# A hybrid decoder block on one core: the query and key products in plain form, and four smaller moves in the order of the work

## The chip, the core and the metric

One core of a Trainium2 chip. The metric is the device time of one launch in microseconds (us); lower is better. Several runs are made of a kernel, and their median is its time. The profiled execution is one more run, taken by the hardware profiler. TensorE is written PE here, VectorE DVE, ScalarE ACT, GpSimd POOL, and SP is the engine that issues most DMAs.

## The reference

One layer on 1024 tokens of width 1024, all float32:

- `u = rmsnorm(x)`, then one projection `z = u @ w_in` whose columns are cut into latents for attention (384 for queries, 256 for keys and values, 32 for a rotary key), queries and keys of gated linear attention (GLA; 256 columns each, 4 heads of 64), GLA values (512), a decay of rank 16, an output gate (512) and two branch gates `gate_a`, `gate_b` (1024 each).
- Branch A is causal attention with 8 heads: the latents are normalised by rmsnorm and projected up to queries, keys and values, part of them with rotary positions; softmax; then `w_o`.
- Branch B is GLA: `log_a = log_sigmoid(g_lr @ w_gate2 + b_gate) / 16`, a running sum of `log_a` in chunks, a state carried from chunk to chunk, rmsnorm and a gate `silu(og)`; then `w_o`.
- `h = x + (sigmoid(gate_a) * y_a + sigmoid(gate_b) * y_b) @ w_out`
- `h = h + (silu(u2 @ w_gate) * (u2 @ w_up)) @ w_down` with `u2 = rmsnorm(h)` and an inner width of 2816; the output is `rmsnorm(h)`.

## The kernel before

**Products in three parts.** Each float32 operand is split in a high part (fp32r) and a low part, the rest. `mm3` (L130) makes one product of a 128x128 weight block and 512 tokens with three matmuls of 512 columns: high by high, high by low, low by high (lines L132 to L134). A split is one copy on ACT (L160) and one subtraction, most on DVE (L161).

**Pairs with seven products.** `pair` (L255) handles 256 columns of `w_in`. The weight is cut in four blocks (two column halves, two halves of the 1024 rows), and the tokens in two halves. Instead of the eight products of blocks it makes seven, from sums of weight blocks and of token blocks: `p_first`, `p_t2`, `p_second`, `p_t3`, `p_t1`, `p_t4`, `p_last` (L200 to L244). One product is `bprod`, four chunks of `mm3`, so 12 matmuls; a pair has 84. The sums of weight blocks and the recombination of results are DVE operations of 128x512 in between. The token sides are the tiles `T["B11"]`, `"B21"`, `"B22"` (blocks) and `"T1"` to `"T4"` (sums), made once at the start and kept for every pair.

**The start** (L271 to L361). x comes in eight tiles of 128 tokens. Each is normalised (`norm_in`: ACT square, DVE, POOL power, DVE), turned by PE (`turned`, four transposes into a PSUM bank of tag "g", of which there are four), and evicted with ACT and DVE into high and low parts. `ONE` (queries) and `TWO` (keys) are the first two pairs, written out here so that their products lie between the steps that build the token sides. Their kept results use a tag `early` of their own.

**After it**, in program order: a pair for the decay columns and half the key latent (`load_lr`), the log decay (L412 to L449), the GLA values (`values_gla`, seven products of 48 matmuls with 256 columns), the GLA units (two halves of the tokens by two pairs of heads, a chain over ACT, POOL, DVE and PE), eight pairs (query latent, output gate, `gate_a`) that fill PE beside the GLA chain, then `gp.close()`, which gives back GLA's memory. Behind it, in memory that was GLA's, `latents` and `token_rows` (L732 to L789) normalise the two latents: squares on ACT, sums on DVE, matmuls with one column (L753), a power on POOL, row scales spread by PE (L766), then splits on ACT and DVE. Three of the four `gate_b` pairs stand behind the latents (L803), the last one beside the work that prepares attention.

**The order** on each engine is set when the kernel is built: a planner places instructions by program order as priority, with its own durations, as soon as it believes their inputs and a buffer to be there. On the chip each engine takes its list in order, and so a late instruction holds up all behind it. Buffers of a tag are handed out in the same way: the weight splits (`ws`) and the raw latents (`wc`) share tags `wh` and `wl`, four each; raw weights are `wr`, four; staging tiles `st`, five.

**The down projection** (L1371 to the end) again makes seven products, of 11 chunks. Its activations come back from memory (`load_x`, tile `xr`, in the pool `dp`, which lies where the token sides `T2`, `T3`, `T1`, `B22` of the feed-forward part were), its weights through `load_y` (tiles `dr` in the pool `r4` with 14 slots, `y` in `dp`). `ordered_load` (L1117) ties all these loads into one order on SP. The results of the last feed-forward pair are stored from ACT's queue (`pair_out`, L1267).

Of the kernel before, what the change touches and what calls it, by code (L numbers as in the profile page):

```python
# [48 lines left out]
def block_kernel(ctx, tc, x, positions, ln_mix, w_in, norm_cq, w_uq, norm_ckv, w_ukv, w_oa,  # L49
# [129 lines left out]
    def columns(off):  # L179

        def load(raw, j):
            nc.sync.dma_start(raw, win[j * HALF:(j + 1) * HALF, off:off + 256].rearrange("(c p) n -> p c n", p=P))
        return load

    def weights(load, tiles=None):
        raw = [(tiles() if tiles else wraw(D)).rearrange("p (c n) -> p c n", c=4) for j in range(2)]
        for j in range(2):
            load(raw[j], j)
        return {f"A{i + 1}{j + 1}": raw[j][:, :, i * P:(i + 1) * P] for i in range(2) for j in range(2)}
# [7 lines left out]
        for c in range(4):  # L197
            mm3(ps, a[:, 0, c], a[:, 1, c], *T[b][c], first and c == 0, last and c == 3)

    def p_first(w, tiles=sttile):  # L200
        w["a"] = bank()
        w["tiles"] = tiles
        bprod(w["a"], sp(w["A11"]), "B11", True, True)
        w["U2"] = tiles()
# [14 lines left out]
    def p_t3(w):  # L219
        minus(w["A12"], w["A12"], w["A11"])  # L220
        minus(w["A11"], w["A11"], w["A22"])
        ps = bank()
        bprod(ps, sp(w["A11"]), "T3", True, True)
        w["U3"] = w["tiles"]()
        plus(w["U3"], w["U2"], ps)

    def p_t1(w, out):
# [43 lines left out]
    with ExitStack() as s1:  # L271
        xpool = pool("xpool", side="right", c=s1)

        def load_x(t):
            xt = xpool.tile([P, D], F32, name="xt", tag="xt", bufs=8)
            nc.sync.dma_start(xt, x2[t * P:(t + 1) * P, :])
            return xt

        def norm_in(xt):
            ssq = small.tile([P, 1], F32, name="ssq", tag="ssq")  # L280
            jk = sttile().bitcast(BF16)
            nc.scalar.activation(jk, xt, AF.Square, accum_out=ssq)
# [5 lines left out]
        def turned(xn, c):  # L288
            ps = bank("g")
# [4 lines left out]
        def early():  # L294
            return xpool.tile([P, HALF], F32, name="early", tag="early", bufs=4)


        raw0 = [parts(v4(F32)) for c in range(4)]
        xs0 = [load_x(t) for t in range(4)]
        ONE = weights(columns(O_GQ))  # L300
        xs1 = [load_x(t) for t in range(4, 8)]
        TWO = weights(columns(O_GK))
        xn = [norm_in(xt) for xt in xs0]
        for c in range(KC):
            j, k = divmod(c, 4)
            hi, lo = T[("B11", "B21")[j]][k]
            gc = g_mix[:, c:c + 1]
            ps = turned(xn, c)
            nc.scalar.activation(hi, ps, AF.Copy, scale=gc)
            nc.vector.scalar_tensor_tensor(lo, ps, gc, hi.bitcast(F32), ALU.mult, ALU.subtract)  # L310
            nc.scalar.activation(raw0[k][j], ps, AF.Copy, scale=gc)
        out_q = store(d_q, (0, P), scale=0.125)
        out_k = store(d_k, (0, P))
        p_first(ONE, early)
        xn = [norm_in(xt) for xt in xs1]
        p_second(ONE, out_q)
        p_first(TWO, early)
        p_second(TWO, out_k)

        T["T2"] = [parts(v4()) for c in range(4)]  # L320
        T["B22"], T["T1"] = ([parts(uslot(1)) for c in range(4)] for i in range(2))
        T["T4"] = [parts(k4(F32R)) for c in range(4)]
        t12, t4 = [], []

        def split2(dst, src):
            nc.scalar.copy(dst[0], src)
            minus(dst[1], src, dst[0].bitcast(F32))

        for c in range(4):
            g0, g1 = g_mix[:, c:c + 1], g_mix[:, c + 4:c + 5]  # L330
            T1, T2 = parts(xpool.tile([P, D], F32, name="t12", tag="xt", bufs=8))
            t12.append((T1, T2))
            p12 = turned(xn, c)
            nc.vector.scalar_tensor_tensor(T1, p12, g0, raw0[c][0], ALU.mult, ALU.subtract)
            p22 = turned(xn, c + 4)
            nc.vector.scalar_tensor_tensor(T2, p22, g1, T1, ALU.mult, ALU.subtract)
            hi, lo = T["B22"][c]
            nc.scalar.activation(hi, p22, AF.Copy, scale=g1)
            nc.vector.scalar_tensor_tensor(lo, p22, g1, hi.bitcast(F32), ALU.mult, ALU.subtract)
            split2(T["T2"][c], T2)  # L340
        for w in (ONE, TWO):
            p_t2(w)
        T["T3"] = [parts(v4()) for c in range(4)]
        for c in range(4):
            T3, T4 = parts(xpool.tile([P, D], F32, name="t34", tag="xt", bufs=8))
            t4.append(T4)
            minus(T3, raw0[c][0], t12[c][1])
            minus(T4, raw0[c][1], t12[c][1])
            split2(T["T3"][c], T3)
        for w in (ONE, TWO):  # L350
            p_t3(w)
        for c in range(4):
            split2(T["T1"][c], t12[c][0])
        for w, o in ((ONE, out_q), (TWO, out_k)):
            p_t1(w, o)
        for c in range(4):
            split2(T["T4"][c], t4[c])
        for w, o in ((ONE, out_q), (TWO, out_k)):
            p_last(w, o)
        for w, o in ((ONE, out_q), (TWO, out_k)):  # L360
            p_t4(w, o)  # L361

    gp = ExitStack()
    g = pool("gla", side="right", c=gp)
# [48 lines left out]
    for i in range(4):  # L413
        ps = bank("g")
        for j in range(2):
            t = 2 * i + j
            nc.tensor.matmul(ps[:, j * 256:(j + 1) * 256], glr[t // 4][0:17, (t % 4) * P:(t % 4 + 1) * P],
                             wg2[0:17, :], start=True, stop=True)
        ab = g.tile([P, HALF], F32, name="lab", tag="E", bufs=2)
        nc.scalar.activation(ab, ps, AF.Abs)  # L420
        nc.scalar.activation(ab, ab, AF.Exp, scale=-1.0)
        if i % 2 == 0:
            la2 = g.tile([P, S], F32, name="la", tag="A", bufs=2)
        l = la2[:, (i % 2) * HALF:(i % 2 + 1) * HALF]
        nc.vector.tensor_scalar(l, ps, 0.0, None, ALU.min)
        la.append((ab, l))
        nc.scalar.activation(ab, ab, AF.Ln, bias=1.0)
        nc.vector.tensor_tensor(l, l, ab, ALU.subtract)
    def gb_tile():
# [21 lines left out]
    def values_gla():  # L451
        A = {}
        for nm, i, j in (("A11", 0, 0), ("A21", 1, 0), ("A22", 1, 1), ("A12", 0, 1)):
            if nm == "A12":
                t = g.tile([P, D], F32, name="a12", tag="A", bufs=2)
            else:
                t = wraw(D)
            A[nm] = t.rearrange("p (c n) -> p c n", c=4)
            nc.sync.dma_start(A[nm], win[j * HALF:(j + 1) * HALF, O_GV + i * 256:O_GV + (i + 1) * 256]
                              .rearrange("(c p) n -> p c n", p=P))  # L460
# [235 lines left out]
        pair(columns(O_GA + i * 256), store(d_ga, (i * 256, i * 256 + P)))  # L696
    gp.close()
    pair(columns(O_GA + 768), store(d_ga, (768, 896)))


    m1x = ctx.enter_context(ExitStack())
# [98 lines left out]
                         start=True, stop=True)  # L800
        kr_ps.append(ps)

    for i in range(3):  # L803
        pair(columns(O_GB + i * 256), store(d_gb, (i * 256, i * 256 + P), AF.Sigmoid))


    ROT = (slice(64, 128), slice(0, 64))
# [566 lines left out]
    NC = NPAIR  # L1374
    IN_R4 = 5

    def load_x(c, nm):
        i, k = XPOS[nm]
        t = dp.tile([P, HALF], F32, name="xr", tag="xr", bufs=9)
        ordered_load(t, d_a[c][i][:, k * HALF:(k + 1) * HALF])  # L1380
        return t

# [19 lines left out]
        return [pbank("B", 4) if k else pbank("AD"[t // 2], 2) for t in range(4)]  # L1402

    def chunk(ps, c, xname, y, tiles=range(4)):
        s = unit_split(load_x(c, xname))
        t = unit_split(y)
        chunk_mm(ps, c, s, t, tiles)
        return s, t
# [43 lines left out]


    b0 = newbanks(0)
    for c in range(IN_R4):
        load_y(c, 0)
    for c in range(NC):
        if c + IN_R4 < NC:
# [98 lines left out]
```

## Time and profile before

| | us |
|---|---|
| median of 3 runs | 1538.72 |
| lowest, highest | 1534.5, 1540.16 |
| the profiled execution, its own time | 1534.73 |
| its span | 1533.0 |
| PE busy in the span | 1462.6 (95%) |
| DVE, ACT, POOL busy | 1030.8, 675.8, 458.8 |
| mean granted PE clock | 0.982 of full speed |

Times inside the span are counted from its start. The profiled run is one execution; outside its span lie 1.7 us. "Busy" is the share of time in which an engine has an instruction running, and a line number is that of the kernel before.

### The profile page before, as it was taken

How to read it: one execution, taken by the hardware profiler on the slowest of the kernel's cores; microseconds unless marked ns; L12 is line 12 of the kernel's file. 1: busy time of each engine (PE TensorE's matmuls, PEld its weight loads, DVE VectorE, ACT ScalarE, POOL GpSimd, SP SyncE). 2: the span in 40 equal slices, each digit the busy share in tenths (PEclk: the TensorE clock that was granted, in tenths of full speed). 3: DMA queues.
4: the chain of work that ended last, by engine and by line, in shares of the span. 5: the costliest groups of instructions: out<-in, count | busy, mean ns of one | idle time of the engine just before them, and what ended most of it. 6: DMA issues, size and time to landing. Idle time of an engine off the chain costs nothing.

```text
span 1533.0 us, 20365 instructions
## 1 busy us (share of the span) xinstructions
PE 1462.6 (95%) x7430; PEld 1216.7 (79%) x7430; DVE 1030.8 (67%) x1483; ACT 675.8 (44%) x1334; POOL 458.8 (30%) x406
## 2 busy tenths in 40 slices
PE   6889999999799999999999989999999999799997
PEld 4679887788588888887899868888888888688886
DVE  7837885887655768566622776666666666786775
ACT  7443345643535767566411732222222223354454
POOL 2100231222101224233821455555555555100000
PEclk9899999999799999999999999999999999999999
DMA  6223324234242013356742213333322334943461
GB/s 191 76 90 112 117 76 137 84 96 150 64 130 78 9 35 105 110 178 211 251 152 83 83 48 100 101 103 103 104 95 97 103 103 160 384 136 97 132 198 55
DMA packets 121110, 181.51 MB, mean 118 GB/s; under 512 B 12897, under 2 KB 74866, under 8 KB 121010
## 3 DMA queue, kind: packets, MB, share of 16 engines
q1 hardware_dynamic: 120434, 178.38, 35.3%
q10 hardware_dynamic: 576, 1.84, 0.3%
q8 instruction: 58, 0.95, 0.3%
q14 instruction: 42, 0.34, 0.1%
HBM read 125.66 MB, written 54.53 MB: 118 GB/s over the span
## 4 chain that ended last, share of the span: by engine, by line
PE 50%; DVE 3%; DMA 0%; ACT 0%; POOL 0%; issue 0%; DVEq 0%; ACTq 0%; POOLq 0%
PE psB L133 6%; PE psB L134 6%; PE psB L132 6%; PE psA L132 5%; PE psD L132 5%; PE psD L133 5%; PE psD L134 5%; PE psA L133 5%; PE psA L134 5%; PE psy L134 1%; PE psy L133 1%; PE psy L132 1%; DVE UT L161 0%; DMA d_h<-h 0%; DVE h L1152 0%; DVE raw L1346 0%
## 5 line engine op out<-in xcount | busy, mean ns | idle before, releaser
L161 DVE TENSOR_TENSOR ws<-wr,ws 128x512 fp32r<-128x512 f32 x149 | 140.7, 957 | 23.5 <-ACT ws L160 23.0
L160 ACT CAST ws<-wr 128x512 fp32r<-128x512 f32 x171 | 103.0, 622 | 92.0 <-PE ps_mm L134 38.6
L132 PE MATMUL ps_mm<-u,ws 128*128 128x512 f32 x240 | 98.0, 411 | 6.6 <-ACT st L205 5.0
L133 PE MATMUL ps_mm<-u,ws 128*128 128x512 f32 x240 | 97.6, 407 | 1.0 <-DVE u L310 1.0
L134 PE MATMUL ps_mm<-u,ws 128*128 128x512 f32 x240 | 96.6, 404 | 0.0
L161 POOL TENSOR_TENSOR ws<-sS,ws 128x512 fp32r<-128x512 f32 x44 | 70.7, 1616 | 68.7 <-ACT ws L160 68.7
L95 POOL TENSOR_TENSOR rx<-rs_m,nhalf 128x1 f32<-128x1 f32 x24 | 14.1, 595 | 257.0 <-DVE rs_m L94 255.5
L160 ACT CAST ws<-xr 128x512 fp32r<-128x512 f32 x77 | 47.3, 621 | 88.0 <-PE psB L134 39.3
L1205 ACT COPY p<-psA 128x512 f32<-128x512 f32 x22 | 12.9, 587 | 157.0 <-PE psA L134 157.0
L612 POOL TENSOR_TENSOR X<-E,gk 128x512 f32<-128x512 f32 x28 | 41.2, 1478 | 136.5 <-ACT E L610 55.2
L161 DVE TENSOR_TENSOR ws<-xr,ws 128x512 fp32r<-128x512 f32 x77 | 52.8, 689 | 39.1 <-ACT ws L160 37.0
L133 PE MATMUL psB<-UT,ws 128*128 128x512 f32 x176 | 69.8, 397 | 2.4 <-DVE UT L161 2.4
L132 PE MATMUL psA<-UB,ws 128*128 128x512 f32 x176 | 69.7, 396 | 0.7 <-ACT p L1205 0.7
L132 PE MATMUL psB<-UT,ws 128*128 128x512 f32 x176 | 69.8, 396 | 0.1
L134 PE MATMUL psB<-UT,ws 128*128 128x512 f32 x176 | 69.6, 395 | 0.0
L134 PE MATMUL psA<-UB,ws 128*128 128x512 f32 x176 | 69.5, 395 | 0.0
L133 PE MATMUL psA<-UB,ws 128*128 128x512 f32 x176 | 69.3, 394 | 0.0
L176 DVE TENSOR_TENSOR st<-st,ps_mm 128x512 f32<-128x512 f32 x75 | 51.3, 685 | 26.6 <-PE ps_mm L134 24.1
L934 DVE TENSOR_TENSOR ws<-pspt,ws 128x512 fp32r<-128x512 f32 (+1 forms) x80 | 49.7, 632 | 17.4 <-ACT ws L933 16.9
L132 PEld LDWEIGHTS ps_mm<-u,ws 128*128 128x128 f32 x240 | 46.2, 192 | 18.4 <-ACT st L205 5.1
L915 ACT ACTIVATE u<-pss,nb 128x128 f32<-128x128 f32 (+3 forms) x64 | 47.8, 746 | 24.3 <-DVE nb L913 14.1
L160 ACT CAST ws<-sS 128x512 fp32r<-128x512 f32 x88 | 50.2, 619 | 16.9 <-DVE sS L1181 16.9
(450 smaller groups left out, 4671.6 us busy)
## 6 DMA issues: line engine op xcount, KB each, us to landing
xr<-d_a SPq DMA_DIRECT2D x77, 256.0 KB, 3.0
wr<-in_w_in_dram SPq DMA_DIRECT2D x31, 512.0 KB, 4.1
wr<-in_ffn_w_gate_dram SPq DMA_DIRECT2D x22, 512.0 KB, 3.8
wr<-in_ffn_w_up_dram SPq DMA_DIRECT2D x22, 512.0 KB, 3.7
d_a<-p SPq DMA_DIRECT2D x20, 512.0 KB, 2.9
dr<-in_ffn_w_down_dram SPq DMA_DIRECT2D x14, 512.0 KB, 8.4
d_a<-R SPq DMA_DIRECT2D x10, 512.0 KB, 2.6
xt<-in_x_dram SPq DMA_DIRECT2D x8, 512.0 KB, 9.1
```

Of the source, the lines that this page charges most:

```text
L95: nc.gpsimd.tensor_tensor(dst, m, nhalf[:, :n], ALU.pow)
L132: nc.tensor.matmul(ps, ah, bh, start=first, stop=False, **kw)
L133: nc.tensor.matmul(ps, ah, bl, start=False, stop=False, **kw)
L134: nc.tensor.matmul(ps, al, bh, start=False, stop=last, **kw)
L160: nc.scalar.copy(dst[:, 0], src)
L161: (lo_eng or nc.gpsimd).tensor_tensor(dst[:, 1], src, dst[:, 0].bitcast(F32), ALU.subtract)
L176: plus = lambda d, x, y: nc.vector.tensor_tensor(d, x, y, ALU.add)
L612: nc.gpsimd.tensor_tensor(X, E, k, ALU.mult)
L915: nc.scalar.activation(pt[:, 0:w], ps[:, 0:w], AF.Exp, bias=bias, accum_out=sums[h // 2][:, t, e:e + 1])
L934: nc.vector.tensor_tensor(tl[:, 0:w], ps[:, 0:w], th[:, 0:w].bitcast(F32), ALU.subtract)
L1205: nc.scalar.copy(tt[:, 0:HALF], psA)
```

## The change

Five edits:

1. **Queries and keys.** `ONE` and `TWO` go. `begin` loads 128 columns of `w_in` at a time (four loads: two for queries, two for keys), splits the whole 128x1024 block at once, and makes the plain product for the first token half (`proj`: 8 chunks, 24 matmuls); the same weights are kept, and make the product for the second half later. A new token side `B12` (the first 512 rows of the second token half) is split for it. The sums `T1` to `T4` are still made, for the pairs that follow. The transposes of the first four chunks use PSUM banks of tag "mm".
2. **Log decay.** The four `Ln` stand in a loop of their own behind the four `Abs` and `Exp`; two of the four buffers are of tag `gk`.
3. **`values_gla`** takes block `A12` from the tag `wr`, as the other three, and no longer from GLA's tag `A`.
4. **Latents.** Two of the `gate_b` pairs go ahead of the latents, right behind the last `gate_a` pair; one stays behind.
5. **Down.** The first four activation tiles of the first product come into two slots of `r4` (`xf`) and are loaded alternately with the first weights.

```diff
-        ONE = weights(columns(O_GQ))
...
-        p_first(ONE, early)
-        xn = [norm_in(xt) for xt in xs1]
-        p_second(ONE, out_q)
-        p_first(TWO, early)
-        p_second(TWO, out_k)
...
+        T["B12"] = [parts(k4(F32R)) for c in range(4)]
+        first = []
+        def proj(w, half):
+            ps = bank()
+            for c in range(KC):
+                j, k = divmod(c, 4)
+                mm3(ps, w[0][:, c, :], w[1][:, c, :], *T[f"B{j + 1}{half + 1}"][k], c == 0, c == KC - 1)
+            return ps
+        def begin(off, out, e):
+            w = wload(win[:, off:off + P], KC, P, nc.vector)
+            out(e, 0, proj(w, 0), True)
+            first.append((w, out, e))
+        def turned_split(dst, ps, gc):
+            nc.scalar.activation(dst[0], ps, AF.Copy, scale=gc)
+            nc.vector.scalar_tensor_tensor(dst[1], ps, gc, dst[0].bitcast(F32), ALU.mult, ALU.subtract)
...
+        xn = [norm_in(load_x(t)) for t in range(4)]
+        for c in range(KC):
+            ps = turned(xn, c, "mm" if c < 4 else "g")
+            turned_split(T[("B11", "B21")[j]][k], ps, gc)
+            nc.scalar.activation(raw0[k][j], ps, AF.Copy, scale=gc)
+        begin(O_GQ, out_q, 0)
+        begin(O_GQ + P, out_q, 1)
+        xn = [norm_in(load_x(t)) for t in range(4, 8)]
+        begin(O_GK, out_k, 0)
         for c in range(4):
             p12 = turned(xn, c)
+            turned_split(T["B12"][c], p12, g0)
             nc.vector.scalar_tensor_tensor(T1, p12, g0, raw0[c][0], ALU.mult, ALU.subtract)
             p22 = turned(xn, c + 4)
+            turned_split(T["B22"][c], p22, g1)
             nc.vector.scalar_tensor_tensor(T2, p22, g1, T1, ALU.mult, ALU.subtract)
-        for w in (ONE, TWO):
-            p_t2(w)
+        begin(O_GK + P, out_k, 1)
+        T["T2"] = [parts(v4()) for c in range(4)]
+        for c in range(4):
+            split2(T["T2"][c], t12[c][1])
+        for (w, out, e) in first:
+            out(e, 1, proj(w, 1), True)
...
-        for w in (ONE, TWO):
-            p_t3(w)
...
-        ab = g.tile([P, HALF], F32, name="lab", tag="E", bufs=2)
+        ab = g.tile([P, HALF], F32, name="lab", tag=("E", "gk")[i // 2], bufs=2)
...
+    for ab, l in la:
         nc.scalar.activation(ab, ab, AF.Ln, bias=1.0)
         nc.vector.tensor_tensor(l, l, ab, ALU.subtract)
...
-            if nm == "A12":
-                t = g.tile([P, D], F32, name="a12", tag="A", bufs=2)
-            else:
-                t = wraw(D)
+            t = wraw(D)
...
     gp.close()
     pair(columns(O_GA + 768), store(d_ga, (768, 896)))
+    for i in range(2):
+        pair(columns(O_GB + i * 256), store(d_gb, (i * 256, i * 256 + P), AF.Sigmoid))
...
-    for i in range(3):
-        pair(columns(O_GB + i * 256), store(d_gb, (i * 256, i * 256 + P), AF.Sigmoid))
+    pair(columns(O_GB + 512), store(d_gb, (512, 640), AF.Sigmoid))
...
+        if nm == "11" and c < 4:
+            if c % 2 == 0:
+                x_first.append(slot("xf"))
+            t = x_first[-1][:, (c % 2) * HALF:(c % 2 + 1) * HALF]
+        else:
+            t = dp.tile([P, HALF], F32, name="xr", tag="xr", bufs=9)
...
     for c in range(IN_R4):
+        if c < 4:
+            ahead_x[c] = load_x(c, "11")
         load_y(c, 0)
```

## Rows read from the trace of the kernel before

**Rows 1.** Page, parts 1 and 2: busy us; PE's busy tenths in 40 slices.
```profile
PE 1462.6 (95%) x7430; PEld 1216.7 (79%) x7430; DVE 1030.8 (67%) x1483; ACT 675.8 (44%) x1334; POOL 458.8 (30%) x406
...
PE   6889999999799999999999989999999999799997
```
**Rows 2.** Stretches, us: busy of PE, PEld, DVE, ACT, POOL; clock; DMA share; GB/s.
```profile
0.00:20.00 20.00, 9.76 (x30) 6.77 (x31) 10.30 (x21) 14.17 (x24) 4.46 (x14) 1.00 0.94 315
...
40.00:60.00 20.00, 16.36 (x52) 12.02 (x51) 20.00 (x34) 9.77 (x19) 1.85 (x4) 0.78 0.00 0
...
100.00:120.00 20.00, 13.10 (x77) 11.96 (x76) 9.03 (x15) 18.52 (x25) 1.27 (x2) 0.76 0.10 27
120.00:140.00 20.00, 20.00 (x167) 19.49 (x167) 15.61 (x18) 8.25 (x13) 1.72 (x2) 0.98 0.45 140
```
**Rows 3.** The same view, of the stretches around the latents.
```profile
385.00:395.00 10.00, 6.93 (x45) 5.58 (x43) 3.19 (x9) 5.03 (x17) 3.25 (x5) 0.93 0.24 70
395.00:405.00 10.00, 7.12 (x20) 4.91 (x20) 10.00 (x17) 7.51 (x14) 1.51 (x2) 0.50 0.09 35
405.00:415.00 10.00, 5.78 (x14) 4.39 (x15) 9.31 (x18) 4.65 (x9) 2.02 (x1) 0.54 0.00 0
```
**Rows 4.** Chain of waits, entry to the down projection: start us, us, what.
```profile
1305.25 0.25 PE psD L134
...
1309.57 1.78 POOL p L1265
...
1311.74 0.63 ACT ws L160
1312.41 0.80 PE psA L132
```
**Rows 5.** Stretches as in rows 2, right behind that entry.
```profile
1310.00:1315.00 5.00, 2.59 (x6) 2.11 (x7) 3.79 (x6) 2.31 (x4) 1.34 (x1) 0.50 0.82 263
```
**Rows 6.** PE in order of time, first and last of 20 matmuls: start us, us.
```profile
60.10 0.40 PE L133 MATMUL ps_mm<-u,ws 128*128 128x512 f32 x1
...
64.53 0.40 PE L134 MATMUL ps_mm<-u,ws 128*128 128x512 f32 x1
```
**Rows 7.** PE in order of time around the log decay.
```profile
97.89 3.72 PE L417 MATMUL ps_g<-wg,glr 17*128 17x256 f32 x16
...
118.44 0.41 PE L132 MATMUL ps_mm<-wh,v 128*128 128x256 f32 x1
```
**Rows 8.** Groups by line, PE, 0 to 98 us: busy us, mean ns, idle before.
```profile
L291 PE MATMUL ps_g<-ident,xt 128*128 128x128 f32 x64 | 12.1, 338 | 11.5 <-DVE rs_m L94 8.7 <-DVE u L339 2.0 <-DVE t L334 0.4
```
**Rows 9.** Groups by line, DVE, 0 to 98 us.
```profile
L161 DVE TENSOR_TENSOR ws<-wr,ws 128x512 fp32r<-128x512 f32 x21 | 13.9, 689 | 0.0
...
L310 DVE SCALAR_TENSOR_TENSOR u<-ps_g,g_mix,u 128x512 fp32r<-128x512 f32 x8 | 5.7, 746 | 0.0
...
L465 DVE TENSOR_TENSOR wl<-wr,wh 128x1024 fp32r<-128x1024 f32 x2 | 2.5, 1226 | 6.1 <-PE ps_mm L134 4.4 <-issue 1.6
```
**Rows 10.** Groups by line, ACT, 0 to 120 us.
```profile
L427 ACT ACT_TABLE_LOAD x4 | 5.1, 1283 | 0.1
...
L421 ACT ACT_TABLE_LOAD x3 | 3.8, 1283 | 0.1
...
L421 ACT ACTIVATE lab<-lab 128x512 f32<-128x512 f32 x4 | 2.5, 631 | 0.1
...
L609 ACT ACT_TABLE_LOAD x1 | 1.3, 1283 | 0.0
```
**Rows 11.** Who waited for whom, PE, 385 to 420: us, times, longest.
```profile
PE ps_mm L132 <- ACT st L205: 5.0, 1, 5.0
```
**Rows 12.** Tile wc, 300 to 420: ns min/median/max, first and last start.
```profile
L738 SPq DMA_DIRECT2D wc<-d_c x5: 319/320/456, 345.0 to 361.2; - x5
```
**Rows 13.** Who waited for whom, SP's queue, 1280 to 1340.
```profile
SPq L1119 <- DMA d_a<-R: 8.0, 1, 8.0
```
**Rows 14.** Groups by line, ACT, whole span: table loads at the stores' function.
```profile
L267 ACT ACT_TABLE_LOAD x3 | 3.8, 1283 | 0.1
```

More of the change, by code (lines that the diff above doesn't have):

```diff
@@ L198, in bprod, with p_first @@
             mm3(ps, a[:, 0, c], a[:, 1, c], *T[b][c], first and c == 0, last and c == 3)
-    def p_first(w, tiles=sttile):
+    def p_first(w):
         w["a"] = bank()
-        w["tiles"] = tiles
         bprod(w["a"], sp(w["A11"]), "B11", True, True)
-        w["U2"] = tiles()
+        w["U2"] = sttile()
         nc.scalar.copy(w["U2"], w["a"])
@@ L223, in p_t3 @@
         bprod(ps, sp(w["A11"]), "T3", True, True)
-        w["U3"] = w["tiles"]()
+        w["U3"] = sttile()
         plus(w["U3"], w["U2"], ps)
@@ L286, in norm_in, with turned @@
             return xt
-        def turned(xn, c):
-            ps = bank("g")
+        def turned(xn, c, tag="g"):
+            ps = bank(tag)
             for i in range(4):
@@ L292, in turned @@
             return ps
[L294 to L299, printed above, removed]
-        ONE = weights(columns(O_GQ))
[L301 to L313, printed above, removed]
-        p_first(ONE, early)
-        xn = [norm_in(xt) for xt in xs1]
-        p_second(ONE, out_q)
-        p_first(TWO, early)
-        p_second(TWO, out_k)
[L320 to L323, printed above, removed]
+        T["B22"] = [parts(uslot(1)) for c in range(4)]
+        T["B12"] = [parts(k4(F32R)) for c in range(4)]
[10 more added lines that the diff above has]
+            first.append((w, out, e))
         def split2(dst, src):
@@ L327, in split2 @@
             minus(dst[1], src, dst[0].bitcast(F32))
+        def turned_split(dst, ps, gc):
+            nc.scalar.activation(dst[0], ps, AF.Copy, scale=gc)
+            nc.vector.scalar_tensor_tensor(dst[1], ps, gc, dst[0].bitcast(F32), ALU.mult, ALU.subtract)
+        out_q = store(d_q, (0, P), scale=0.125)
+        out_k = store(d_k, (0, P))
+        raw0 = [parts(v4(F32)) for c in range(4)]
+        xn = [norm_in(load_x(t)) for t in range(4)]
+        for c in range(KC):
+            j, k = divmod(c, 4)
+            gc = g_mix[:, c:c + 1]
+            ps = turned(xn, c, "mm" if c < 4 else "g")
[5 more added lines that the diff above has]
+        begin(O_GK, out_k, 0)
+        t12, t4 = [], []
         for c in range(4):
@@ L333, in block_kernel @@
             p12 = turned(xn, c)
+            turned_split(T["B12"][c], p12, g0)
             nc.vector.scalar_tensor_tensor(T1, p12, g0, raw0[c][0], ALU.mult, ALU.subtract)
             p22 = turned(xn, c + 4)
+            turned_split(T["B22"][c], p22, g1)
             nc.vector.scalar_tensor_tensor(T2, p22, g1, T1, ALU.mult, ALU.subtract)
[L337 to L340, printed above, removed]
-        for w in (ONE, TWO):
-            p_t2(w)
+        begin(O_GK + P, out_k, 1)
[4 more added lines that the diff above has]
+            out(e, 1, proj(w, 1), True)
+        T["T1"] = [parts(uslot(1)) for c in range(4)]
         T["T3"] = [parts(v4()) for c in range(4)]
@@ L349, in block_kernel @@
             split2(T["T3"][c], T3)
-        for w in (ONE, TWO):
-            p_t3(w)
         for c in range(4):
             split2(T["T1"][c], t12[c][0])
-        for w, o in ((ONE, out_q), (TWO, out_k)):
-            p_t1(w, o)
+        T["T4"] = [parts(k4(F32R)) for c in range(4)]
         for c in range(4):
             split2(T["T4"][c], t4[c])
[L358 to L361, printed above, removed]
     gp = ExitStack()
@@ L1375, in block_kernel @@
     IN_R4 = 5
+    x_first = []
     def load_x(c, nm):
         i, k = XPOS[nm]
-        t = dp.tile([P, HALF], F32, name="xr", tag="xr", bufs=9)
+        if nm == "11" and c < 4:
[4 more added lines that the diff above has]
+            t = dp.tile([P, HALF], F32, name="xr", tag="xr", bufs=9)
         ordered_load(t, d_a[c][i][:, k * HALF:(k + 1) * HALF])
@@ L1404, in chunk @@
     def chunk(ps, c, xname, y, tiles=range(4)):
-        s = unit_split(load_x(c, xname))
+        s = unit_split(ahead_x.pop(c) if xname == "11" and c in ahead_x else load_x(c, xname))
         t = unit_split(y)
@@ L1454, in block_kernel @@
     b0 = newbanks(0)
+    ahead_x = {}
     for c in range(IN_R4):
+        if c < 4:
+            ahead_x[c] = load_x(c, "11")
         load_y(c, 0)
```

## The prediction

> **What bounds the kernel now.** I read the page first. PE is busy 1462.6 of 1533.0 us, and no other engine is above 67% [rows 1]: the kernel is bound by PE, and without a cut in PE's own work only the 70.4 us in which PE is idle, and the stretches at half clock, can be won. The 40 slices, of 38.3 us each, show where: the first three, the 11th, the 24th, the 35th and the last [rows 1]. The 24th, from 881 us, and the last are touched by no edit; each of the others lies at one. The view by stretches then gives each hole its size. From 0 to 20 us PE is idle 10.24 us; from 40 to 60 it is idle 3.64 at a mean clock of 0.78, while DVE is busy 20.00 of 20; from 100 to 120 it is idle 6.90 at 0.76, with ACT busy 18.52; from 120 to 140 it is full [rows 2]. Around the latents, 385 to 415, it is idle 3.07 + 2.88 + 4.22 = 10.2 us, and from 395 on the clock is 0.50 to 0.54, so at half speed [rows 3]. At the entry to the down projection the chain of waits goes from the last product of the feed-forward part (ends 1305.50) over POOL's L1265 and ACT's split L160 to the first down product at 1312.41: 6.9 us without PE [rows 4], and 0.50 behind it [rows 5]. Four of the five edits stand at exactly one of these holes, so each is priced from its own.
>
> **Plain products for queries and keys.** 20 matmuls of 512 columns in a row start from 60.10 to 64.53, so one follows another after 4.43 / 19 = 0.233 us [rows 6]. Two pairs have 2 x 84 = 168 matmuls, four plain column blocks 4 x 48 = 192: PE gets 24 x 0.233 = 5.6 us more work. What it gets back is the time lost before the log decay. That begins at 97.89 us with L417 [rows 7]. Until then PE makes 3 x 84 = 252 matmuls (58.8 us), 64 transposes (12.1 us as modelled [rows 8]; some of it is latency) and 19 short products of the values (about 2.2 us): 73 us of work, 25 us lost. Of that PE waits 8.7 us for the normalisation of x, nearly all of it for the first tile [rows 8]; that stays. Of the other 16 us DVE is the main cause: its sums, differences and recombinations stand ahead of each product. DVE loses 14 splits of 512, 8 weight sums and 10 recombinations, 32 x 0.689 = 22.0 us, and gets 4 splits of 1024 at 1.226 and 4 low parts of B12 at 0.746, 7.9 us [rows 9]: 14 us less, on the engine that was full. Moreover the first 72 matmuls of queries and keys need the first token half only, so 16.8 us of PE work lie ready while DVE and ACT make the second half. I expect that 13 to 14 of the 16 us go. Net: -13.5 + 5.6 = -8 us. What is late next is ACT: 16 evictions of the first half, each about as long as a split, pace the first plain product. Bounds: -11 if all of it goes, +6 if the hole only moves, so that just the added work is left. The weight loads move as many bytes with rows half as long, in a stretch where the DMA share is 0.94 [rows 2]; at worst they take twice as long, and the +6 holds that. Hidden: the split weights hold all of `wh` and `wl` until the second half is through, so the first split of the next pair waits for the first of four such products; the other three, 72 x 0.233 = 16.8 us, cover a split of about 1.3 us. Without that cover it would cost 1.3. `T4` now waits for B12's buffers, but is wanted five products (14 us) into the next pair.
>
> **Log decay by function.** Each Exp and each Ln takes its own table here: 4 + 3 loads inside and 1 behind, 1.283 us each, with nothing of ACT's idle between [rows 10]. By function it takes one load to Ln and one back: six fewer, 6 x 1.283 = 7.7 us. PE's side gives the same: from L417 to the first product that doesn't wait (118.44) it is 20.55 us [rows 7]; with the change L417's first quarter is done after 3.72 / 4 = 0.9, and then come 8 Abs and Exp and 4 Ln (12 x 0.63), a load, a subtraction of 0.7 and a last group of short matmuls (2, an estimate), in all 12.4 [rows 7, 10]. That is 8.1 less; I take -7.5, since a few of PE's short products lay in the hole and still have to be made. Bounds: -10 (the half clock goes too), 0 if the planner sets Ln between the Exps all the same. The `k` tile of the first GLA unit now waits for the last two of the four buffers, and SP's later loads stand behind that load; the running sums, their copies and the first exponent lie in between and hide it, else +2. A rule of the Trainium skill speaks against the edit (ScalarE: Activation LUTs, section Table sets: the hidden batching unit): one set holds both exp and ln, so that grouping them would save nothing beyond one load. By it this edit gives 0 to -2.6. The trace differs: seven loads stand between the four Exps and the four Lns [rows 10].
>
> **`A12` from another tag.** It no longer waits for the log decay's tile. But PE is 20.00 of 20 busy from 120 to 140 [rows 2], so nothing waited for it: 0. The next pair's weights now find no free `wr`; seven products of the values, 7 x 48 matmuls of half the length (39 us), hide their load; else one load, about 4 us.
>
> **Latents behind two gate pairs.** Their raw rows are loaded from 345 to 361 us, yet the chain (squares, sums, power, scales, splits) runs from 390 on, in memory that GLA gives back, with no pair left beside it: in 395 to 405 DVE is full and PE not [rows 3]. The longest wait, 5.0 us, is for a copy of the next pair's first result, which stood in ACT's list behind the latents' splits [rows 11]. With two pairs ahead, 2 x 84 x 0.233 = 39 us of products cover some 25 us of chain; DVE needs 16 operations per pair (7 splits, 4 sums, 5 recombinations) and 24 for the latents, 56 x 0.689 = 38.6 us [rows 9], so it only just fits, and what is left over falls to the third pair. Lost here: 10.2 idle plus up to half of the 12.9 us that PE is busy at half clock, 16.6 in all. I take -11: the tail of GLA stays, and buffers are shared, since the five raw rows hold five of eight `wh`/`wl` from 345 to 361 us on [rows 12]. Bounds: -14, and +3 if the pairs ahead starve for those buffers. Behind it only two pairs instead of four cover the work toward attention; what is moved is work that had slack there, so 0.
>
> **First down operands in `r4`.** The wait goes over ACT: the split of the first `xr` stands behind stores in ACT's list that wait for POOL (1309.57 + 1.78, then 1311.74) [rows 4]. Tiles that come early let the planner put their splits ahead of those stores, as it did for the weights. Then two chunks, 24 x 0.233 = 5.6 us, can run from 1305.5 on, and the next split still comes at about 1311.7: some 1.5 us of the 6.9 stay, and the half clock behind it (6 matmuls at nearly twice the time, 1.3 us) goes. SP is next: it waited 8.0 us for a store of that pair [rows 13], and now two more slots of the 14 are asked for early, so a weight load, and all ordered behind it, can wait for a token side to come free. I leave 1.2 us for that: -5.5. Bounds: -8.2 (all of it), +5 if the loads are late as a whole.
>
> **Sum.** -8 - 7.5 - 0 - 11 - 5.5 = -32 us. On the profiled run's own time that is 1534.7 - 32 = 1502.7; the median of the runs is 4.0 above it, so 1538.7 - 32 = 1506.7. I say 1507 us.
>
> **Rivals.**
> 1. *The early hole only moves.* ACT, at 14.17 of 20 in the first 20 us [rows 2], becomes the bound, the plain products wait for its evictions, and edit 1 gives +4 instead of -8. 1519 us. For it: ACT has all evictions, the squares and the wide casts at once. Against: in 40 to 60 us ACT has half its time free [rows 2]. Chance 0.12.
> 2. *The cover is too thin at the latents.* The raw rows hold the split buffers, and the two pairs run at the pace of the three left; edit 4 gives 0. 1518 us. For it: five loads at 345 to 361 for use behind 390 [rows 12]. Against: in the 10th slice, 345 to 383 us, they were held too, and PE is at 9 [rows 1]. Chance 0.13.
> 3. *The down entry keeps its wait*: the planner still sets the stores first, or the loads are late. 1512 us, or 1517 with the bad bound. Chance 0.10, inside my range.
> 4. *The other side: table loads among GLA's exponents.* Two Sigmoid pairs have 8 stores through the function; drawn forward into the last GLA units, each can cost two loads, 2.57 us, on ACT in GLA's chain, 8 x 2.57 = 20.5, and again on the Squares and Exps that wait for DVE behind them, up to twice that. From 32 us, so 12 or 13 alternations on the path, the kernel is slower; at all of them, 1548 us. Against: the six pairs with functions before, 24 stores, needed 3 loads in all [rows 14]. Chance 0.05.
> 5. *One table for both functions*: then no load at all would be left, another 2 x 1.283 = 2.6 us, 1504. The seven loads between Exps and Lns speak against it [rows 10]. Chance 0.02. The Trainium skill (ScalarE: Activation LUTs, Table sets: the hidden batching unit) states such a set.
>
> **Numbers.** Forecast 0.58, rivals as given. Its own range adds the spread of the terms: 1496 to 1518. Rivals 1 to 3 reach to 1519, two of them at once to 1530. Below, all the good bounds together (-11, -10, -14, -8.2) give 1495.5, and the spread of the runs 4 more. Range 1490 to 1528, which leaves out about 0.05 below and 0.1 above. Within 0.5% of 1538.7 is within 7.7 us, about what a measurement of this kernel can tell from no change. Faster than that: forecast and rivals 1 to 3 and 5 but for 0.06 in which several fail together, so 0.89; the same 0.06; slower 0.05.
>
> **What would show it.** Step 1: L417 starts near 90 us instead of 97.9, DVE below 20.00 in 40 to 60, and 192 matmuls ahead of the next pair. Step 2: two table loads between the first Abs and the first GLA exponent, and no wait of PE over 2 us there. Step 4: no copy wait of 5 us, and a clock of 1.00 where the latents run. Step 5: a split of `xf` ahead of the stores on ACT, and a first down product within 2 us of the last feed-forward one. I am wrong if PE's idle time falls by less than 15 us in sum, or if a new hole of over 5 us stands between 40 and 120 us.

## The result and the profile after

1515.25 us (median of 4 runs, 1512.22 to 1516.4), beside 1537.37 us for the kernel before in the same comparison: ratio 0.9853, 95% interval [0.9828, 0.9878], so 22 us less. The profiled run took 1514.89 us with a span of 1513.2 us, 19.8 less than the span before.

Page of the kernel after, parts 1 and 2, as in [rows 1]:

```profile
PE 1456.1 (96%) x7454; PEld 1214.8 (80%) x7454; DVE 1017.8 (67%) x1459; ACT 673.3 (44%) x1329; POOL 464.0 (31%) x406
...
PE   6999999999979999999999899999999999899997
```

PE's idle time fell from 70.4 to 57.1 us, by 13.3. The other 6.5 us of the 19.8 are busy time, although 24 matmuls (5.6 us) came in: matmuls that ran at half clock before run at full clock now (mean granted clock 0.982 before, 0.989 after). Of the slices named before, the second and third are filled and the 35th is fuller; the 11th was traded for the 12th, and the stretches show that the first is emptier. Stretches of the kernel after, as in [rows 2] and [rows 3]:

```profile
0.00:20.00 20.00, 6.25 (x34) 5.75 (x35) 10.44 (x18) 13.97 (x22) 4.14 (x14) 0.96 0.95 304
...
40.00:60.00 20.00, 20.00 (x105) 16.55 (x104) 15.47 (x24) 10.52 (x18) 3.18 (x15) 1.00 0.07 28
...
100.00:120.00 20.00, 18.64 (x145) 18.22 (x144) 12.08 (x17) 14.32 (x20) 2.98 (x2) 0.90 0.23 72
```
```profile
385.00:395.00 10.00, 10.00 (x50) 8.32 (x49) 1.40 (x5) 3.69 (x14) 2.20 (x5) 1.00 0.50 172
395.00:405.00 10.00, 10.00 (x46) 8.04 (x45) 5.49 (x9) 5.66 (x10) 0.00 (x0) 1.00 0.67 226
405.00:415.00 10.00, 9.63 (x47) 7.24 (x46) 6.70 (x11) 5.38 (x10) 1.65 (x1) 1.00 0.09 36
415.00:425.00 10.00, 7.04 (x38) 5.62 (x36) 10.00 (x18) 8.40 (x15) 0.00 (x0) 0.99 0.16 57
425.00:435.00 10.00, 3.08 (x5) 1.83 (x6) 8.85 (x17) 2.34 (x4) 2.02 (x1) 0.50 0.49 156
```

From 385 to 415, where PE was idle 10.2 us and at half clock, it is now idle 0.4 us, at clock 1.00; from 415 to 435 it is idle 9.9 us. Who waited for whom (PE, 0 to 140 us, then 385 to 440; before: [rows 8], [rows 11]):

```profile
PE ps_mm L290 <- DVE rs_m L94: 8.3, 1, 8.3
PE ps_mm L132 <- ACT v L329: 5.5, 1, 5.5
PE ps_g L441 <- DVE la L431: 1.4, 1, 1.4
```
```profile
PE ps_mm L132 <- ACT st L204: 9.6, 1, 9.6
```

**The early hole.** ACT in order of time, kernel after:

```profile
13.92 2.42 ACT L316 ACTIVATE u<-ps_mm,g_mix 128x512 fp32r<-128x512 f32 x4
16.20 2.44 ACT L316 ACTIVATE u<-ps_g,g_mix 128x512 fp32r<-128x512 f32 x4
18.49 2.48 ACT L329 ACTIVATE v<-ps_mm,g_mix 128x512 f32<-128x512 f32 x4
```

The first four transposes now stand in the `mm` banks. Those banks come free only with the raw copies (L329), and these stand in ACT's list behind all eight high parts. So the first plain product starts at 19.28 us, with some 14 matmuls at half clock behind it. From 20 to 100 us PE is idle only 0.7 us; the log decay starts at 94.32 us instead of 97.89 [rows 7], with 28 short value products done before it instead of 19.

**The log decay.** ACT, groups by line, 0 to 120 us (before: [rows 10]):

```profile
L430 ACT ACT_TABLE_LOAD x3 | 3.8, 1283 | 0.1
...
L423 ACT ACT_TABLE_LOAD x2 | 2.6, 1283 | 0.0
...
L609 ACT ACT_TABLE_LOAD x1 | 1.3, 1283 | 0.0
```

Six loads instead of eight, not two: the planner set Ln between the Exps all the same. Yet PE's wait there fell from 6.9 to 1.4 us. The loads are not all of it. PE, kernel after:

```profile
103.24 0.41 PE L132 MATMUL ps_mm<-wh,v 128*128 128x256 f32 x1
103.45 0.41 PE L133 MATMUL ps_mm<-wl,v 128*128 128x256 f32 x1
```

First, the short products in front of the sums run at half clock in this profile, 0.21 us apart (granted clock 0.61 from 100 to 105 us), and so cover more of the wait; in a kernel below with the same early code (the order at the latents) they run 0.12 us apart, and PE waits 4.2 us. Second, more of them stand there: the first product of `v` comes at 103.24 us instead of 118.44 [rows 7]. This goes with the third edit, `A12` from another tag, and not with the first: the six kernels without it, plain products or not, load `A12` at 104 to 114 us, have 19 short products ahead of the log decay, and the first product of `v` at 111 to 119; all eight with it load `A12` by 78.5 us, have 28, and the first product of `v` at 96 to 103. How the one leads to the other wasn't traced further.

**The latents.** SP's queue and ACT in order of time, kernel after:

```profile
416.32 0.33 SPq L726 DMA_DIRECT2D wr<-in_mla_w_ukv_dram  x1
423.78 1.64 SPq L182 DMA_DIRECT2D wr<-in_w_in_dram  x2
```
```profile
427.47 0.62 ACT L160 CAST ws<-wr 128x512 fp32r<-128x512 f32 x1 [3.28 <-DMA wr<-in_w_in_dram]
430.76 0.62 ACT L160 CAST ws<-wr 128x512 fp32r<-128x512 f32 x1 [2.67 <-DMA wr<-in_w_in_dram]
431.29 0.58 ACT L204 COPY st<-ps_mm 128x512 f32<-128x512 f32 x1
```

The copy that PE waits for, of the third gate pair's first product, stands in ACT's list behind two splits of the last pair's weights. Those were loaded at 423.78 us, since all four `wr` buffers were taken by the pair before, the rotary key rows and the up projections.

**The down entry.** ACT, kernel after (before: [rows 4]):

```profile
1278.11 0.62 ACT L160 CAST ws<-xf 128x512 fp32r<-128x512 f32 x1 [5.87 <-DMA xf<-d_a]
...
1285.57 0.62 ACT L160 CAST ws<-xf 128x512 fp32r<-128x512 f32 x1
1288.88 0.34 ACTq L1270 DMA_DIRECT2D d_a<-R  x1
```

All four `xf` splits stand ahead of the first store; the first down product starts at 1284.67, inside the last feed-forward products. What is left are three waits (PE, 1270 to 1340):

```profile
PE psA L132 <- ACT ws L160: 2.5, 2, 1.3
PE psA L134 <- DVE ws L161: 1.9, 1, 1.9
```

### The profile page after: what moved, and what is told of

Its sections match the earlier page's. It is cut to its first block, busy times and chain, and to the rows that moved or that the text cites. A ratio compares the mean times of both kernels' runs of the same rounds, so it can differ in the third digit from the quotient of the medians.

```text
span 1513.2 us, 20379 instructions
## 1 busy us (share of the span) xinstructions
PE 1456.1 (96%) x7454; PEld 1214.8 (80%) x7454; DVE 1017.8 (67%) x1459; ACT 673.3 (44%) x1329; POOL 464.0 (31%) x406
## 4 chain that ended last, share of the span: by engine, by line
PE 49%; DVE 3%; DMA 1%; issue 0%; ACT 0%; POOL 0%; DVEq 0%; POOLq 0%
PE psB L133 6%; PE psB L134 6%; PE psB L132 6%; PE psA L132 4%; PE psA L134 4%; PE psD L134 4%; PE psD L132 4%; PE psD L133 4%; PE psA L133 4%; PE psy L134 1%; PE psy L132 1%; PE psy L133 1%; DMA xr<-d_a 1%; DMA dr<-in_ffn_w_down_dram 0%; DVE UT L161 0%; DMA d_h<-h 0%
## 5 line engine op out<-in xcount | busy, mean ns | idle before, releaser
L161 DVE TENSOR_TENSOR ws<-wr,ws 128x512 fp32r<-128x512 f32 x135 | 128.3, 960 | 15.5 <-ACT ws L160 14.9
L160 ACT CAST ws<-wr 128x512 fp32r<-128x512 f32 x157 | 94.2, 617 | 64.6 <-DVE wr L177 25.7
L132 PE MATMUL ps_mm<-u,ws 128*128 128x512 f32 x208 | 84.5, 407 | 10.9 <-ACT st L204 10.3
L134 PE MATMUL ps_mm<-u,ws 128*128 128x512 f32 x208 | 83.3, 404 | 0.0
L133 PE MATMUL ps_mm<-u,ws 128*128 128x512 f32 x208 | 83.1, 399 | 0.0
L132 PEld LDWEIGHTS ps_mm<-u,ws 128*128 128x128 f32 x208 | 39.4, 189 | 20.7 <-ACT st L204 10.8
```

Source lines behind the costliest of these rows:

```text
L132: nc.tensor.matmul(ps, ah, bh, start=first, stop=False, **kw)
L133: nc.tensor.matmul(ps, ah, bl, start=False, stop=False, **kw)
L134: nc.tensor.matmul(ps, al, bh, start=False, stop=last, **kw)
L160: nc.scalar.copy(dst[:, 0], src)
L161: (lo_eng or nc.gpsimd).tensor_tensor(dst[:, 1], src, dst[:, 0].bitcast(F32), ALU.subtract)
```

## The experiments

### Each edit alone on the kernel before

Each is that part of the diff shown ahead of the prediction, and nothing else.

**Plain products.**


> The kernel before with the plain query and key products alone. The prediction's term: 8 us less (DVE was what cost PE the time, 13 to 14 us of it come back, 5.6 us of matmuls are added). Rival, from the trace after: the gain at the log decay is only 3.6 us on the clock (97.89 to 94.32 us, with nine short value products more already done, about 2 us), because a new wait of 5.5 us for a PSUM bank and some fourteen matmuls at half clock stand in front of the first plain product. It gives 4 to 6 us less, and the bank wait of about 5.5 us stands in this kernel's trace too.

1529.36 us, ratio 0.9939 [0.9923, 0.9955]: 9.4 us less. That is what the prediction had; the trace shows the rival's wait. In the profiles the gain is less: the first attention score starts at 496.9 us instead of 500.7, 3.8 earlier (the profiled run of the kernel before, 1534.73 us, is itself 3.6 below the median of its 29 runs here). The bank wait stands here too, and the log decay still waits 5.3 us:

```profile
PE ps_g L440 <- DVE la L430: 5.3, 3, 3.2
PE ps_mm L132 <- ACT v L329: 4.4, 1, 4.4
```

**Log decay by function.**


> The kernel before with the log decay's loop split by function alone. The prediction's term: 7.5 us less, with two table loads between the first Abs and the first GLA exponent. Its bad bound, that the planner mixes the functions all the same: 0. From the trace after (six loads instead of eight, yet PE waits only 1.4 us there): the gain doesn't come from the loads, and by them it should be 2 x 1.283 = 2.6 us; if PE's waits of 6.9 us go as they did in the kernel after, 5 to 7 us.

1536.82 us, 0.9989 [0.9979, 0.9999]: 1.7 us less (0.2 to 3.2 by the interval): the two saved loads, 2.6 us, fit; the 7.5 predicted and the 5 to 7 read from PE's waits do not. Six loads, as in the kernel after. The wait fell from 6.9 to 4.2 us only:

```profile
PE ps_g L439 <- DVE la L429: 4.2, 2, 2.8
```

**Two gate pairs ahead.**


> The kernel before with the two gate pairs ahead of the latents alone. The prediction's term: 11 us less. Rival, from the trace after: the hole only moves, from the wait of 5.0 us beside the latents to one of about 9.6 us behind them, where ACT's list holds a copy behind splits of weights that were loaded late; by that 3 to 6 us less, all of it from the clock and the small holes at the latents. The moved wait should be seen in this kernel too.

1534.64 us, 0.9977 [0.9964, 0.9989]: 3.5 us less, as the rival had it, with the moved wait:

```profile
PE ps_mm L132 <- ACT st L205: 9.5, 1, 9.5
```

From 385 to 445 us PE is busy 49.99 us, beside 49.82 in the same 60 us before: the idle time was kept whole. What was won is clock: 0.95 on average over these 60 us, beside 0.83 before.

**First down operands.**


> The kernel before with the first down operands in the other pool alone. The prediction's term: 5.5 us less. Rival, from the trace after, where from the last feed-forward product to the end 3.7 us were won: 3 to 4 us less, the wait of 6.9 us gone and two waits of about 1.3 us and a stretch at half clock some 20 us later in its place.

1534.37 us, 0.9973 [0.9961, 0.9986]: 4.2 us less. Waits of PE from 1270 to 1345 us:

```profile
PE psA L132 <- ACT ws L160: 3.6, 2, 2.4
PE psA L134 <- DVE ws L161: 2.0, 1, 2.0
```

**Plain products and log decay together.** Both parts of the diff, run last.


> The kernel before with the plain products and the log decay by function, nothing else. Alone they brought 9.4 and 1.7 us, the four edits alone 18.8 us, all five together 22.6. If the two depend on each other, as POOL's copies and the ordered Ln did in the kernel after, they bring 13 to 16 us together (ratio 0.990 to 0.991) and close the sum. If they only add: 11 us (0.993), and the other 4 us lie elsewhere, with the fifth edit or between the gate pairs and the rest.

1534.4 us, 0.9975 [0.9961, 0.9989]: 3.8 us less, so neither. The four alone come to 18.8 us, all five edits to 22.6 by their ratio, which the intervals don't tell apart, but these two bring less together than the 9.4 and 1.7 alone. The traces show a part of where it goes. The first GLA output (`go`) stands at 231.5 us before, 227.0 with the plain products, 226.8 with the log decay, 222.4 with both: there the gains add to 9.1 us. At the first attention score 3.2 are left. But there the two alone have 3.8 and -0.1, so up to that point only 0.5 us is lost by putting them together; what is lost is the gain of the log decay, and it is lost alone as well. Another 4.6 us between this profile and that of the plain products alone lie in the attention stage (last section), and whether the edits have to do with that isn't shown. Stretches of this kernel:

```profile
360.00:380.00 20.00, 15.66 (x77) 12.65 (x76) 13.53 (x22) 5.90 (x13) 1.27 (x1) 0.91 0.22 68
380.00:400.00 20.00, 13.26 (x63) 9.67 (x63) 11.05 (x24) 12.52 (x37) 6.15 (x8) 0.77 0.15 52
```

PE is idle 4.3 and 6.7 us there (0 and 3.7 before, 0 and 5.2 with the plain products alone, 1.7 and 4.8 with the log decay alone). The last GLA output moved by only 4.0 us (393.6 to 389.6), and the pairs beside GLA were used up sooner. In the kernel after PE is full from 360 to 400: the two gate pairs ahead are the work that takes up what the early edits win. At the first attention score the three edits alone come to -3.8 + 0.1 - 3.5 = -7.2 us, the kernel after to -17.2 (483.5). That the pairs are the reason is read from the traces. The third edit, not run alone, is the other difference there that could matter: without it, PE waits 6.0 us at the log decay in this kernel, beside 1.4 in the kernel after, and 4.2 in the one with the same early code whose short products ran at full clock.

```profile
PE ps_g L441 <- DVE la L431: 6.0, 2, 3.3
```

### The three mechanisms on the kernel after

**Banks freed by the split.**

```
-            nc.scalar.activation(raw0[k][j], ps, AF.Copy, scale=gc)
+            nc.gpsimd.tensor_tensor(raw0[k][j], *(t.bitcast(F32) for t in T[("B11", "B21")[j]][k]), ALU.add)
```


> The kernel after, with the raw copies of the first token half made by POOL from the two split parts in SBUF, not by ACT from PSUM, so that a bank is free as soon as its split is done. Theory: the wait of 5.5 us ahead of the first plain product is for a bank that ACT's raw copy frees only behind all eight high parts; then the first plain product starts near 15 us instead of 19.28 and the kernel is 3 to 5 us shorter, ratio to the kernel before 0.982 to 0.983. Rival (the prediction's view, ACT's evictions pace the product): the first product waits for the last of the high parts all the same, starts after 18 us, and the time stays that of the kernel after, ratio 0.985.

1514.5 us, 0.9849 [0.9832, 0.9866]: no gain beside 0.9853. But the mechanism holds: the wait is gone (1.2 us, for DVE), PE is busy 10.39 us in the first 20 instead of 6.25, and the log decay starts at 88.3 us, 6 earlier. A part is given back at once: from the first matmul of the log decay to its last sum PE has 27 short products instead of 52, and its wait for the sums is longer:

```profile
PE ps_g L441 <- DVE la L431: 4.3, 2, 2.8
PE ps_mm L132 <- DVE u L317: 1.2, 1, 1.2
```

The first GLA output still comes 6.1 us earlier (216.6 beside 222.7), the last 5.3 (392.6 beside 397.9), but the first attention score only 1.7 (481.8 beside 483.5). PE is idle 10.3 us from 400 to 440 as in the kernel after; how the rest is lost on the way isn't shown. The expectation took the gain at one hole for a gain at the end.

**Ln last.** `after_` sets an order in one engine's list, without a wait:

```
+        last_exp = nc.scalar.activation(ab, ab, AF.Exp, scale=-1.0)
...
+        after_(nc.scalar.activation(ab, ab, AF.Ln, bias=1.0), last_exp)
```


> The kernel after, with each Ln of the log decay ordered behind the last Exp in ACT's list. The trace must show two table loads between the first Abs and the first GLA exponent, not six. Theory: with value products beside it the log decay no longer sets PE's pace, PE waited 1.4 us there and ran some 5 us at half clock; 1 to 3 us less than the kernel after, ratio 0.983 to 0.985. Rival (the prediction's pricing): each load is a load on the path, 4 x 1.283 = 5.1 us less, ratio 0.982.

1513.56 us, 0.9845 [0.9826, 0.9864]: 1.2 us, not told apart from none; in its profile the first attention score is 3.4 earlier, but the attention stage 2.9 longer (last section). Two loads, as ordered, and no wait of PE at the log decay any more:

```profile
L435 ACT ACT_TABLE_LOAD x1 | 1.3, 1283 | 0.0
L614 ACT ACT_TABLE_LOAD x1 | 1.3, 1283 | 4.4 <-DVE E L613 4.4
```

One load stands between the last Exp and the first Ln, so in this build the two are not served by one table. The Trainium skill (ScalarE: Activation LUTs, section Table sets: the hidden batching unit) states a set with both; the trace differs, and it decides here.

**Both.**


> The kernel after with POOL's raw copies and with each Ln behind the last Exp, the two that alone brought 0.6 and 1.2 us. Theory: the first moves the start of the log decay 6 us forward, but then PE has fewer value products to lay beside ACT's table loads and gives it back there; the second takes that wait away. Together 5 to 8 us less than the kernel after, ratio 0.980 to 0.982, and the log decay starts near 88 us with no wait for its subtraction. Rival: the two are independent and add, about 2 us, ratio 0.984, and the gain of the kernel with all three came from the third.

1507.79 us, 0.9805 [0.9785, 0.9825]: 7.4 us less than the kernel after, where each alone brought next to nothing. The log decay starts at 88.3 us and PE doesn't wait for it. At the first attention score the two come 1.7 and 3.4 us earlier alone, 9.1 together (474.4), which speaks for two holes that depend on each other; between the medians the excess over the sum, 5.6 us, isn't clear of their spread. The wait of 4.3 us that the copies alone ran into is gone, as the expectation has it; that it accounts for all of the excess isn't shown.

**Weights of the last gate pair first.**

The last pair's `weights` is called ahead of both loads, and these follow it on SP:

```
+    after_(nc.sync.dma_start(krr, d_c[640:704, :]), loads[-1])
...
+            after_(nc.sync.dma_start(raw, w_ukv[0][c * P:(c + 1) * P, :]), loads[-1])
```


> The kernel after, with the loads of the rotary key rows and of the up projections ordered on SP's queue behind the weights of the last gate pair, so that these weights find free wr buffers. Theory: the 9.6 us without PE behind the latents come from those weights, loaded at 423.8 and 425.0 us because wr was full, and from their splits standing in ACT's list ahead of the copy that PE waits for; the hole falls under 3 us and the kernel is 6 to 10 us shorter, ratio 0.979 to 0.981. Rival: the work of the latents on DVE (88 to 100% busy from 415 to 435 us) and ACT sets the hole, and it only takes another name; less than 2 us, ratio 0.984 or more. Against the theory too: the up projections' splits, now loaded later, could themselves hold ACT's list.

1516.68 us, 0.9865 [0.9848, 0.9882]: nothing won. The wait changed its name, as the rival said, but not for the rival's reason alone. PE, then ACT:

```profile
PE ps_g L776 <- DVE st L773: 8.5, 2, 8.1
```
```profile
428.26 0.62 ACT L736 CAST wh<-wr 128x512 fp32r<-128x512 f32 x1 [5.20 <-DMA wr<-in_mla_w_ukv_dram]
428.78 1.13 ACT L160 CAST ws<-wr 128x512 fp32r<-128x512 f32 x2
429.82 0.58 ACT L212 COPY st<-ps_mm 128x512 f32<-128x512 f32 x1
```

The weights are there in time, but now the up projections' split, loaded late, holds ACT's list and the copy (429.82 instead of 431.29). And PE's own list has a product that spreads the queries' row scales (L776) ahead of the pair's next products; it waits till 430.35 for its diagonal on DVE. Two in-order lists hold PE, with the same end, at 430.4 us.

**All three.**


> The three changes together on the kernel after. If each theory holds and they add: 10 to 18 us less than the kernel after, some 1498 to 1505 us, ratio 0.974 to 0.979. If the early stages only hand their gain to the next wait: little more than the best of the three alone.

1506.55 us, 0.9802 [0.9783, 0.9821]: 7.8 us less than the kernel after, beside 7.4 with the two early ones: nothing told apart from none comes from the loads.

**The order at the latents.** No load is tied to another. The third pair is written ahead of the row scales and the rotary key rows, so that its last weights are loaded at 358 us instead of 374 and these rows at 375 instead of 351, all long before the hole at 422. In ACT's list the splits of the up projections' and of the last pair's weights follow the third pair's copy (`behind` holds it while the last pair's first two products are written); in PE's the row scales and the sums of the rotary key rows follow its second product:

```
+            after_(nc.scalar.copy(hi[:, c], r4_), w3["copy"])
...
+        i = nc.scalar.copy(dst[:, 0], src)
+        if behind:
+            after_(i, behind[0])
...
+    rq_ps = token_rows(sc_q, w3["second"])
```


> The kernel after, with the order set where the hole stands: in ACT's list the copy of the third gate pair's first product goes ahead of the splits of the last pair's and the up projections' weights, and in PE's list the products that spread the queries' row scales and sum the rotary key rows go behind that pair's second product. No load is moved. Theory (from the kernel with the loads moved, where the wait kept its length and changed its name from the copy on ACT to the row scales on DVE): two waits of nearly the same end hold PE, one in ACT's list and one in PE's own; with both behind the pair's products PE has work from 421 us on, the hole falls from 9.6 us to under 3, and the kernel is 6 to 10 us shorter, ratio 0.979 to 0.981. Rival: DVE, 88 to 100% busy there, is what PE waits for, and the pair's products run at DVE's pace; 0 to 3 us, ratio 0.983 or more.

1504.86 us, 0.9787 [0.9766, 0.9808]: 10.1 us less than the kernel after, at the top of what was expected (in the profiles 7.2, by the first attention score). One wait over 0.4 us is left from 380 to 460, with PE busy 18.04 of 20 from 420 to 440 and DVE 18.09. So it was the order of the lists, not DVE's work, although DVE has little time free there; how much each of the two lists brought wasn't taken apart. The wait that is left, and the one at the log decay in this profile:

```profile
PE ps_mm L132 <- ACT ws L167: 1.9, 1, 1.9
```
```profile
PE ps_g L451 <- DVE la L441: 4.2, 2, 2.7
```

**With both early ones.**


> All of it on the kernel after: POOL's raw copies, each Ln behind the last Exp, and the order at the latents. If both holes are what they were taken for: 12 to 17 us less than the kernel after, 1498 to 1503 us, ratio 0.974 to 0.978. If the hole at the latents is DVE's: as the kernel with all three before, ratio 0.980.

1496.07 us, 0.9729 [0.9709, 0.9749]: 19.1 us less than the kernel after, 7.4 + 10.1 and a little more, and the best of all. Its page:

```profile
PE 1449.7 (97%) x7454; PEld 1212.2 (81%) x7454; DVE 1021.8 (68%) x1459; ACT 662.3 (44%) x1315; POOL 478.5 (32%) x414
...
PE   7999999999999999989999899999999999899997
```

## Why the prediction was right, and where it was wrong

The time, 1515, lies 8 us above the 1507 predicted, inside the range and on the predicted side. By one of its own tests, that PE's idle time must fall by 15 us, it failed: 13.3. No new hole of over 5 us stands between 40 and 120 us; the two that count stand outside, at 14 and at 422. That the time came so near is in part luck: two of the four terms that were priced brought a quarter and a third of their price alone, and a range of 38 us holds that.

- *Plain products, -8.* Alone -9.4 by the medians, -3.8 by the profiles at the first attention score. The named cause was right: DVE fell from 20.00 to 15.47 in 40 to 60 us and PE filled up. "What is late next is ACT" was right too, but priced at nothing. It was the bank that ACT frees last, 5.5 us and half clock behind; hence 94.3 instead of "near 90", and 88.3 once that wait was taken away.
- *Log decay, -7.5.* Alone -1.7. The step "one load to Ln and one back" failed: the bad bound, Ln set between the Exps, came true. Whether a load that goes brings its length isn't settled: the two that went fit (2.6 us), the other four, 5.1 by that price, brought 1.2 us in the kernel after and 6.8 on top of POOL's copies, each give or take 4 to 5. PE has 52 products beside the loads in the kernel after, 27 with POOL's copies; that this number sets what a load costs PE is read from the traces, not tested.
- *`A12`, 0.* Not tried alone, so its worth in time is open. But the step to 0 doesn't hold as it was reasoned: it took from PE being full from 120 to 140 us that nothing waited. The traces show that the kernels without this edit lack short products beside the log decay, at the very hole of the term before (19 ahead of it instead of 28, and 26 to 28 beside it instead of 52).
- *Gate pairs ahead, -11.* Alone -3.5. That two pairs cover the chain came true (clock 1.00 from 385 to 415, 0.4 us idle). What failed is "what is left over falls to the third pair", which got no price: 9.6 us fell there, through two lists in which later work stood ahead of the pair's. Rival 2 named the shared buffers and gave the edit 0; the buffers were `wr`, not the split ones, and loading earlier didn't help. What the sum lacked altogether is that the pairs also keep PE busy beside GLA's last units (full from 360 to 400 us, beside 11.1 us idle with the two early edits alone).
- *Down operands, -5.5.* Alone -4.2 [-2.2, -6.0], by the step as described: splits first, then the stores. The 1.5 us left of the wait and the 1.2 for what comes next were too few: 4.4 us of waits in the kernel after, with PE at clock 0.54 from 1305 to 1310, where the half clock was to go.
- *Rival 1* (ACT the bound) came true in its mechanism, not in its price; rivals 4 and 5 didn't come true.

So 8 + 7.5 + 11 + 5.5 = 32 was priced as four separate holes. Alone they gave 18.8; together 22.6, not told apart by the intervals. By the traces, what the early edits win is kept only with the pairs behind it (7.2 us at the first attention score for the three alone, 17.2 together); how much of that is the third edit's isn't known, and 3 to 4 us of any single median may be a wait in the attention stage (last section).

## What to carry to other kernels

A wait that ends at an in-order list is not gone when its cover comes earlier: ask which instruction stands next in that list, on the waiting engine and on the one that frees its buffer, and price that wait. A stretch in which PE is full doesn't show that a late load costs nothing: ask whether its products could have filled a hole before it. Time won early is kept only if there is other work to lay beside the next serial chain, so price neighbouring holes together and not one by one. And where an edit only asks a planner for an order, look at the order it made, or set it.

## What the runs showed of the hardware

The attention stage, the same code in all 14 profiles, has two lengths. From the first score product to the first of the mix it takes 211.3 to 212.3 us in nine of them, 214.1 to 215.9 in five. One wait of PE, some 160 us in, tells them apart: 0.9 to 1.4 us in the nine, 2.5 to 3.2 in the five (the gate pairs alone, the down operands alone, plain products with the log decay, Ln last, and the best kernel). Plain products alone, then plain products with the log decay (waits, then stretches from 660 to 680 us):

```profile
PE pspt L932 <- DVE ws L936: 1.5, 2, 1.2
```
```profile
660.00:680.00 20.00, 18.74 (x119) 15.69 (x118) 14.93 (x24) 13.86 (x32) 9.91 (x8) 1.00 0.65 209
```
```profile
PE pspt L933 <- DVE ws L937: 3.5, 2, 3.2
```
```profile
660.00:680.00 20.00, 16.76 (x93) 14.25 (x92) 13.42 (x19) 11.79 (x26) 9.67 (x7) 0.83 0.64 195
```

Between these two profiles 2 us more of waiting go with a stage 4.6 us longer; the granted clock fell behind the wait (0.83 over these 20 us, with 93 matmuls instead of 119). Which kernel falls into it how often can't be told from one profile each. So 3 to 4 us between two medians of single edits, those of the plain products and of the pair above among them, may be this wait and not the edit.
